# A streamed-weight transformer block on one core: one activation buffer of the MLPs turned into four raw weight tiles and two split pairs

## The chip, the cores and the metric

One core of one Trainium2 chip runs the whole program. The metric is the device time of one execution in microseconds (us), as the median of several runs; lower is better. The engines are TensorE (PE, with PEld for its weight loads), VectorE (DVE), ScalarE (ACT), GpSimd (POOL) and SyncE (SP), and SP's queue issues the weight loads.

## The reference

The input is 256 tokens of width 2048. Layer 0 mixes them with S5 and HGRN2, layer 1 with sliding-window attention, and after each stands an MLP:

```python
def squared_relu_mlp(xn, w_up, w_down):
    return jnp.square(jax.nn.relu(xn @ w_up)) @ w_down

h = x
for layer in range(DEPTH):            # DEPTH = 2
    y = mixer[layer](rms_norm(h, gain[layer]))
    h = h + y
    h = h + squared_relu_mlp(rms_norm(h, mlp_norm[layer]), mlp_w_up[layer], mlp_w_down[layer])
```

`w_up` is 2048 x 8192 and `w_down` 8192 x 2048 in fp32, 64 MB each and twice; together they are two thirds of the 398 MB that the program moves.

## The kernel before

All weights are read once, in one list of **units** that is made before anything runs (`add_units` L80, `add_mlp` L255). A unit is 1024 columns of 128 partitions, 512 KB. Each unit passes three steps:

- its load into a tile `raw` (pool of four, L94), issued by SP at L104, or at L99 where the unit is to be combined with another first;
- its split into two fp32r halves: ACT casts `raw` to `whi` (L129), DVE writes `wlo = raw - whi` (L130); both come from pools of four;
- its matmuls (`mm`, L160), each weight product as hi times hi, hi times lo and lo times hi.

`advance` (L133 to L143) is called once for each unit's matmuls and writes down the loads and splits of later units: loads up to `LOOK_DMA` = 6 units ahead and less than four beyond the last split, splits up to `LOOK` = 3 ahead. The order of each engine's own queue is then set by a scheduler that can put an instruction ahead of others written before it; the waits between engines follow from the tiles. An engine's queue is worked off in order.

The MLP (`mlp` L951) goes through four chunks of 2048 hidden columns. `up(c)` (L971) makes a chunk from 32 units in eight blocks (`ublock`); behind each block ACT and DVE apply the squared ReLU and write the result as a split pair, `ch[c]` with tags `chi` and `clo` (L979 to L986). The pair comes from `new_pair("c")`, which has two buffers, so that chunks alternate. `down(c)` then multiplies the chunk by its rows of `w_down`.

For chunks 0 to 2 `down` is `down_mixed` (L1002), which saves products on part of the work by a seven-product scheme. It follows `down_plan` (L278 to L288), 40 units, which I number idx 0 to 39:

- idx 0 to 17: `t1` (idx 0, 5, 10, 14), `t42` (2, 7, 12, 16) and plain units between them. A `t1` and a `t42` unit have six matmuls each, a plain one 12.
- idx 18 to 31: `b2` (18, 22, 26, 29; six matmuls), `b12` (20, 24, 28, 31; a load of 256 KB, three matmuls) and plain units between them.
- idx 32 to 39: plain units.

That is 84 matmuls of combined units and 24 times 12 = 288 of plain ones, 372 of 512 columns in all. Before the split of a combined unit DVE forms differences on its raw tile (`combine` L108, at L111): one of 512 columns for `t1`, one of 512 and one of 1024 for `t42` (which reads the raw tile of the `t1`), one of 512 for `b12` (which reads that of the `b2`).

Chunk 3 uses `xblock` on 32 plain units. `advance`, `emit_dma`, `emit_split` and `mlp` are what the change touches.

Of the kernel before, what the change touches and what calls it, by code (L numbers as in the profile page):

```python
# [8 lines left out]
F32 = mybir.dt.float32  # L9
F32R = mybir.dt.float32r  # L10
# [7 lines left out]
P = 128  # L18
# [7 lines left out]
LOOK = 3  # L26
WARM = 8
REWARM = 4
LOOK_DMA = 6
# [31 lines left out]
def hybrid_kernel(ctx: ExitStack, tc: tile.TileContext, x, even_norm, even_w_in, s5_lambda_re, s5_lambda_im,  # L61
# [8 lines left out]
    wp = ctx.enter_context(tc.tile_pool(name="wp", bufs=4))  # L70
# [6 lines left out]
    units = []  # L77

    def add_units(W, kts, n0, w=512):
        nk = 1024 // w  # L80
        for i in range(0, len(kts), nk):
            units.append((W, kts[i], n0, nk, None))

    raws, splits = {}, {}
    ptr = {"dma": 0, "split": 0, "use": 0}

    def pieces(i):

        nk = units[i][3]
        return [slice(k, k + 1) for k in range(nk)] if i == 0 else [slice(0, nk)]  # L90

    def emit_dma(i):
        W, kt, n0, nk, kind = units[i]
        raw = wp.tile([P, nk, 1024 // nk], F32, tag="raw", name="raw", bufs=4)  # L94
        raws[i] = raw
        if kind is not None:

            w = 512 if kind == "b12" else 1024
            nc.sync.dma_start(out=raw[:, 0:w // 512], in_=W[kt * P:(kt + 1) * P, n0:n0 + w].rearrange(  # L99
                "p (b n) -> p b n", n=512))  # L100
            return
        src = W[kt * P:(kt + nk) * P, n0:n0 + 1024 // nk].rearrange("(k p) n -> p k n", p=P)
        for ks in pieces(i):
            nc.sync.dma_start(out=raw[:, ks], in_=src[:, ks])  # L104
# [3 lines left out]
    def combine(kind, raw):  # L108

        def sub(o, a, b):  # L110
            V.tensor_tensor(out=o, in0=a, in1=b, op=ALU.subtract)  # L111

        if kind == "t1":
            sub(raw[:, 1], raw[:, 1], raw[:, 0])
        elif kind == "t42":
            sub(raw[:, 0], raw[:, 1], raw[:, 0])
            sub(raw, held["t1"][:, 1:2].to_broadcast([P, 2, 512]), raw)
        elif kind == "b12":
            sub(raw[:, 0], held["b2"][:, 1], raw[:, 0])
        held[kind] = raw  # L120

    def emit_split(i):
        raw, nk, kind = raws.pop(i), units[i][3], units[i][4]
        if kind is not None:
            combine(kind, raw)
        hi = wp.tile([P, nk, 1024 // nk], F32R, tag="whi", name="whi")
        lo = wp.tile([P, nk, 1024 // nk], F32R, tag="wlo", name="wlo")
        for ks in ([slice(0, 1)] if kind == "b12" else pieces(i)):
            S.copy(out=hi[:, ks], in_=raw[:, ks])  # L129
            V.tensor_tensor(out=lo[:, ks], in0=raw[:, ks], in1=hi[:, ks].bitcast(F32), op=ALU.subtract)  # L130
        splits[i] = (hi, lo)

    def advance():  # L133
        i = ptr["use"]
        while ptr["dma"] < min(len(units), i + LOOK_DMA + 1) or ptr["split"] < min(len(units), i + LOOK + 1):
            if ptr["dma"] < min(len(units), i + LOOK_DMA + 1) and ptr["dma"] < ptr["split"] + 4:
                emit_dma(ptr["dma"])
                ptr["dma"] += 1
            else:
                emit_split(ptr["split"])  # L140
                ptr["split"] += 1
        ptr["use"] += 1
        return splits.pop(i)  # L143

# [17 lines left out]
    def wblock(XT, kts, kx=None):  # L162

        acc = psA.tile([P, 4, T], F32, tag="acc", name="acc")
        n = len(kts)
        for i in range(0, n, 2):
            hi, lo = advance()
            for kk in range(2):
                k = kts[i + kk]
                last = i + kk == n - 1  # L170
                for m in range(4):
                    wh, wl = hi[:, kk, m * P:(m + 1) * P], lo[:, kk, m * P:(m + 1) * P]
                    mm(acc[:, m, :], wh, XT.hi[:, k, :], i + kk == 0 and m % 2 == 0, False)
                    mm(acc[:, m, :], wh, XT.lo[:, k, :], False, False)
                    mm(acc[:, m, :], wl, XT.hi[:, k, :], False, last)
            pump(SIDE)
        return acc

    def ublock(XT, kts):

        acc = psA.tile([P, 2, 2, T], F32, tag="acc", name="acc")
        n = len(kts)
        for i in range(0, n, 4):
            hi, lo = advance()
            for kk in range(4):
                k = kts[i + kk]
                for m in range(2):
                    mm(acc[:, m], hi[:, kk, m * P:(m + 1) * P], XT.both[:, :, k, :], i + kk == 0, False)
                for m in range(2):
                    mm(acc[:, m, 0], lo[:, kk, m * P:(m + 1) * P], XT.hi[:, k, :], False, i + kk == n - 1)  # L190
            pump(SIDE)
        return acc
# [42 lines left out]
    def scratch(tag, shape, dtype=F32):  # L235
        return bp.tile(list(shape), dtype, tag=tag, name=tag, bufs=2)
# [14 lines left out]
    for kts in out0_passes:  # L251
        for n in range(4):
            add_units(w_out0, kts, n * 512)

    def add_mlp(l):  # L255
        def up(c):
            for n in range(8):
                add_units(mlp_w_up[l], K16, c * 2048 + n * 256, 256)

        def down(c):  # L260
            if c == 3:
                for n in range(4):
                    add_units(mlp_w_down[l], [c * 16 + k for k in K16], n * 512)
                return
            for kind, n, i in down_plan:
                if kind is None:
                    add_units(mlp_w_down[l], [c * 16 + 2 * i, c * 16 + 2 * i + 1], n * 512)
                else:
                    units.append((mlp_w_down[l], c * 16 + 2 * i + (kind in ("t42", "b2")),
                                  512 if kind == "b12" else 0, 2, kind))  # L270

        for c in range(4):
            up(c)
            down(c)


    NS = 4
# [17 lines left out]
    for kts in out1_passes:  # L295
        for n in range(4):
            add_units(w_out1, kts, n * 512)
    add_mlp(1)


# [40 lines left out]
    for q in range(1, 5):  # L341
        emit_dma(ptr["dma"])
        ptr["dma"] += 1
        load_x(q)
# [17 lines left out]
    for q in range(8):  # L362
        lastx = make_xT(xt, XT0, "g0", 2 * q, 2)
        if q == 0:
            with tc.issue_after(lastx[2].ins):
                for _ in range(REWARM):
                    PE.matmul(wps, warm[:, 0:P], warm, start=True, stop=True, skip_group_check=True)
        if q < 4:
            emit_split(ptr["split"])
            ptr["split"] += 1  # L370
            if q < 3:
                emit_dma(ptr["dma"])
                ptr["dma"] += 1
                load_x(5 + q)
# [576 lines left out]
    def mlp(norm, nxt):  # L951
        XT = norm.XT
        ch, forms = {}, {}
        rst = cp.tile([P, T], F32, tag="rsb", name="rst", bufs=1)

        def row():
# [324 lines left out]
```

## Time and profile before

| what | value |
|---|---|
| median of 3 runs | 2112.44 us (2110.84 to 2113.88) |
| the profiled execution | 2112.92 us |
| its span, first to last instruction | 2110.3 us |
| mean granted TensorE clock | 0.998 |
| PE busy | 2075.3 us (98%) |
| DVE busy | 1481.7 us (70%) |
| ACT busy | 1136.9 us (54%) |
| moved by DMA | 397.75 MB, 188 GB/s over the span |

The profile is of one execution, and sums are made against its own 2112.92 us. Busy times of PE overlap with their neighbours' ends, so a stretch in which PE is busy throughout is told by the rate of its matmuls and by the absence of idle time. Stretches of the span below are called **stages**: an up stage is `up(c)`, a mixed stage is `down_mixed(c)`. The six mixed stages run, by their first matmuls, from 512.40, 694.69, 874.46, 1481.38, 1660.48 and 1839.74 us; the chunk 3 stage of the second MLP is plain and begins at 2019.13 us.

### The profile page before, as it was taken

The page shows a single profiled execution, that of the slowest core. Times are in us where ns is not written, and L with a number is a line of the kernel's source. Part 1 is how long each engine was busy: PE and PEld are TensorE (multiplying, and loading weights), DVE is VectorE, ACT ScalarE, POOL GpSimd, SP SyncE. Part 2 cuts the span into 40 slices and gives each one's busy share as a digit, 9 for nine tenths or more (in the row PEclk, how much of TensorE's full clock was granted, in tenths as well). Part 3 has the DMA queues.
Part 4 walks back from the last instruction along what each step waited for, and adds up shares of the span by engine and source line. Part 5 has one row for each costly group of instructions (what it writes and reads, how often), then busy time and mean ns, then how long its engine had stood idle before and what let it go on. Part 6 is the DMA issues. An engine that isn't in the chain of part 4 may idle for free.

```text
span 2110.3 us, 31236 instructions
## 1 busy us (share of the span) xinstructions
PE 2075.3 (98%) x12144; PEld 1754.9 (83%) x12144; DVE 1481.7 (70%) x2100; ACT 1136.9 (54%) x1541; POOL 38.8 (2%) x38
## 2 busy tenths in 40 slices
PE   9999999999999999999999999999999999999999
PEld 8988988888788878878888888788778878877887
DVE  6799967776666767676655688777767676676654
ACT  5877554565445545544544477565445445544542
POOL 2000000000000000000000110000000000000000
PEclk9999999999999999999999999999999999999999
DMA  8444545566676666566655643456676566567654
GB/s 244 123 150 143 169 159 205 178 182 191 201 223 190 198 231 190 189 220 209 190 189 181 189 149 129 139 175 186 209 230 189 186 230 205 187 214 225 189 200 150
DMA packets 264739, 397.75 MB, mean 188 GB/s; under 512 B 14888, under 2 KB 148560, under 8 KB 264272
## 3 DMA queue, kind: packets, MB, share of 16 engines
q1 hardware_dynamic: 263168, 392.50, 59.0%
q8 instruction: 95, 1.56, 0.3%
q0 software_dynamic: 672, 2.15, 0.3%
q10 hardware_dynamic: 752, 1.12, 0.2%
q14 instruction: 52, 0.43, 0.1%
HBM read 393.62 MB, written 2.10 MB: 188 GB/s over the span
## 4 chain that ended last, share of the span: by engine, by line
PE 78%; DMA 11%; DVE 7%; issue 2%; ACT 2%; SPq 0%; DVEq 0%; ACTq 0%
PE acc L160 65%; PE m L160 12%; DMA raw<-in_mlp_w_down_dram 10%; DVE wlo L130 4%; DVE raw L111 2%; ACT whi L129 1%; PE m L353 1%; PE m L1174 1%; DMA xt<-in_x_dram 0%; DVE t L646 0%; DVE h L1000 0%; PE m L449 0%; DVE clo L986 0%; PE m L1208 0%; ACT chi L627 0%
## 5 line engine op out<-in xcount | busy, mean ns | idle before, releaser
L129 ACT CAST whi<-raw 128x1024 fp32r<-128x1024 f32 (+1 forms) x753 | 777.2, 1036 | 866.8 <-PE acc L160 570.3
L130 DVE TENSOR_TENSOR wlo<-raw,whi 128x1024 fp32r<-128x1024 f32 (+1 forms) x753 | 900.4, 1204 | 443.8 <-ACT whi L129 440.6
L160 PE MATMUL acc<-x,whi 128*128 128x512 f32 (+1 forms) x2816 | 788.1, 366 | 0.2 <-DVE x L357 0.2
L160 PEld LDWEIGHTS acc<-x,wlo 128*128 128x128 f32 x2432 | 458.4, 189 | 91.2
L160 PE MATMUL acc<-x,wlo 128*128 128x256 f32 x2432 | 512.6, 279 | 0.0
L160 PEld LDWEIGHTS acc<-x,whi 128*128 128x128 f32 x2816 | 433.7, 190 | 2.0 <-issue 0.4
L160 PE MATMUL acc<-whi,chi 128*128 128x512 f32 x864 | 338.9, 392 | 0.1
L160 PE MATMUL acc<-wlo,chi 128*128 128x512 f32 x864 | 338.1, 392 | 0.0
L160 PE MATMUL acc<-whi,clo 128*128 128x512 f32 x864 | 338.0, 392 | 0.0
L160 PEld LDWEIGHTS acc<-wlo,chi 128*128 128x128 f32 x864 | 162.6, 188 | 35.4 <-DVE wlo L130 2.0
L160 PEld LDWEIGHTS acc<-whi,chi 128*128 128x128 f32 x864 | 162.3, 188 | 35.5 <-ACT whi L129 1.6
L160 PEld LDWEIGHTS acc<-whi,clo 128*128 128x128 f32 x864 | 162.5, 188 | 33.6
L160 PE MATMUL acc<-whi,x 128*128 128x512 f32 x576 | 181.4, 393 | 0.0
L111 DVE TENSOR_TENSOR raw<-raw 128x512 f32<-128x512 f32 (+1 forms) x96 | 79.1, 824 | 110.9 <-DMA raw<-in_mlp_w_down_dram 110.6
L160 PE MATMUL m<-whi,chi 128*128 128x512 f32 x296 | 112.1, 398 | 14.7 <-ACT whi L129 14.7
L160 PE MATMUL m<-wlo,chi 128*128 128x512 f32 x296 | 116.9, 395 | 9.6 <-DVE wlo L130 9.4
L160 PEld LDWEIGHTS acc<-whi,x 128*128 128x128 f32 x576 | 107.4, 188 | 22.3 <-issue 0.4
L160 PE MATMUL m<-whi,clo 128*128 128x512 f32 x296 | 115.5, 390 | 0.0
L160 PE MATMUL acc<-wlo,x 128*128 128x512 f32 x288 | 113.4, 394 | 0.0
L160 PEld LDWEIGHTS m<-whi,chi 128*128 128x128 f32 x296 | 55.5, 188 | 35.5 <-ACT whi L129 25.1
L160 PEld LDWEIGHTS m<-wlo,chi 128*128 128x128 f32 x296 | 55.6, 188 | 25.5 <-DVE wlo L130 14.7
L160 PE MATMUL m<-whi,forms 128*128 128x512 f32 x192 | 75.3, 392 | 0.0
(243 smaller groups left out, 1560.0 us busy)
## 6 DMA issues: line engine op xcount, KB each, us to landing
raw<-in_mlp_w_down_dram SPq DMA_DIRECT2D x280, 512.0 KB, 4.2
raw<-in_mlp_w_up_dram SPq DMA_DIRECT2D x256, 512.0 KB, 3.7
raw<-in_even_w_in_dram SPq DMA_DIRECT2D x79, 512.0 KB, 3.9
raw<-in_odd_w_qkv_dram SPq DMA_DIRECT2D x40, 512.0 KB, 3.6
raw<-in_even_w_out_dram SPq DMA_DIRECT2D x32, 512.0 KB, 3.9
raw<-in_odd_w_out_dram SPq DMA_DIRECT2D x32, 512.0 KB, 3.8
raw<-in_mlp_w_down_dram SPq DMA_DIRECT2D x24, 256.0 KB, 4.6
raw<-in_s_w_glu_dram SPq DMA_DIRECT2D x8, 512.0 KB, 3.5
```

Source lines behind the costliest of these rows:

```text
L111: V.tensor_tensor(out=o, in0=a, in1=b, op=ALU.subtract)
L129: S.copy(out=hi[:, ks], in_=raw[:, ks])
L130: V.tensor_tensor(out=lo[:, ks], in0=raw[:, ks], in1=hi[:, ks].bitcast(F32), op=ALU.subtract)
L160: PE.matmul(o, a, b, start=start, stop=stop, skip_group_check=True, **kw)
L353: ipe = PE.transpose(ps[:, b, t * P:(t + 1) * P], src[:, t, (a + b) * P:(a + b + 1) * P], ident)
L1174: PE.transpose(ps[:, r, a, :], pr[:, 2 * a + r, k * P:(k + 1) * P], ident)
```

## The change

In an MLP the second buffer of `chi` becomes `more["raw"]`, four raw tiles more, and one buffer of `clo` becomes `more["split"]`, two pairs of split halves more. Units of odd number within the MLP ("home" units) are loaded into the new raw tiles; those whose number is 1 modulo 4 are split into the new pairs. A load may stand ten units ahead (`LOOK_DMA` + 4) and a split five (`LOOK` + 2), as far as their own kind of tile is free. The pair `ch[c]` is left with one buffer. Nothing is computed otherwise.

```diff
+    more = {"from": 0, "end": 0}
+
+    def home(i):
+
+        return more["from"] <= i < more["end"] and i % 2 == 1
+
     def emit_dma(i):
         W, kt, n0, nk, kind = units[i]
-        raw = wp.tile([P, nk, 1024 // nk], F32, tag="raw", name="raw", bufs=4)
+        if home(i):
+            raw = more["raw"][:, i // 2 % 4].rearrange("p (k n) -> p k n", k=nk)
+        else:
+            raw = wp.tile([P, nk, 1024 // nk], F32, tag="raw", name="raw", bufs=4)
         raws[i] = raw
@@ emit_split
-        hi = wp.tile([P, nk, 1024 // nk], F32R, tag="whi", name="whi")
-        lo = wp.tile([P, nk, 1024 // nk], F32R, tag="wlo", name="wlo")
+        if home(i) and i % 4 == 1:
+            hi, lo = [more["split"][:, i // 4 % 2, a].rearrange("p (k n) -> p k n", k=nk) for a in range(2)]
+        else:
+            hi = wp.tile([P, nk, 1024 // nk], F32R, tag="whi", name="whi")
+            lo = wp.tile([P, nk, 1024 // nk], F32R, tag="wlo", name="wlo")
@@ advance
         i = ptr["use"]
-        while ptr["dma"] < min(len(units), i + LOOK_DMA + 1) or ptr["split"] < min(len(units), i + LOOK + 1):
-            if ptr["dma"] < min(len(units), i + LOOK_DMA + 1) and ptr["dma"] < ptr["split"] + 4:
+
+        def room():
+            d = ptr["dma"]
+            if home(d) and d > ptr["split"] + 5:
+                return False
+            return d < min(len(units), i + LOOK_DMA + (4 if home(d) or home(d - 1) else 0) + 1) and sum(
+                home(u) == home(d) for u in raws) < 4
+
+        def ahead():
+
+            u = ptr["split"]
+            if u >= len(units) or u > i + LOOK + 2:
+                return False
+            ext = home(u) and u % 4 == 1
+            return sum((home(v) and v % 4 == 1) == ext for v in splits) < (2 if ext else LOOK + 1)
+
+        while True:
+            if room():
                 emit_dma(ptr["dma"])
                 ptr["dma"] += 1
-            else:
+            elif ahead() and ptr["split"] < ptr["dma"]:
                 emit_split(ptr["split"])
                 ptr["split"] += 1
+            else:
+                break
         ptr["use"] += 1
         return splits.pop(i)
@@ add_mlp: ends.append(len(units)) behind the chunks
@@ mlp
         ch, forms = {}, {}
+        more["raw"] = scratch("chi", [P, 4, 1024])
+        more["split"] = scratch("clo", [P, 2, 2, 1024], F32R)
+        more["from"], more["end"] = ptr["dma"], ends.pop(0)
```

With the change the lines shift: the loads are at L113 and L108, the combine's differences at L120, the subtraction at L142, the matmul at L190, the activation's lines 36 further down.

How the rows of the queues move is shown for the second mixed stage. `raw_N` is a raw tile of the pool, `chi_4782` the four new raw tiles, `clo_4783` the new split pairs, `wlo_N` a pool tile, `m` and `acc` sums in PSUM, `t4` a scratch tile.

SP, loads of that stage, before, idx 3 to 10 of the plan:

```order
L104 DMA raw_6969<-in_mlp_w_down_dram 128x2x512
L104 DMA raw_6992<-in_mlp_w_down_dram 128x2x512
L99 DMA raw_7014<-in_mlp_w_down_dram 128x1024
L104 DMA raw_7051<-in_mlp_w_down_dram 128x2x512
L99 DMA raw_7063<-in_mlp_w_down_dram 128x1024
L104 DMA raw_7082<-in_mlp_w_down_dram 128x2x512
L104 DMA raw_7095<-in_mlp_w_down_dram 128x2x512
L99 DMA raw_7113<-in_mlp_w_down_dram 128x1024
```

And with the change, idx 4, 6, 9, 7, 8, 10, then 13 and 11, then 12, 14:

```order
L113 DMA raw_6814<-in_mlp_w_down_dram 128x2x512
L113 DMA raw_6861<-in_mlp_w_down_dram 128x2x512
L113 DMA chi_4782<-in_mlp_w_down_dram 128x2x512
L108 DMA chi_4782<-in_mlp_w_down_dram 128x1024
L113 DMA raw_6909<-in_mlp_w_down_dram 128x2x512
L108 DMA raw_6961<-in_mlp_w_down_dram 128x1024
L113 DMA chi_4782<-in_mlp_w_down_dram 128x2x512 x2
L108 DMA raw_6994<-in_mlp_w_down_dram 128x1024
L108 DMA raw_7021<-in_mlp_w_down_dram 128x1024
```

Odd units now go to the new tiles, and those that are 1 modulo 4 stand one or two places earlier; a pool tile comes back eight units later instead of four.

DVE in the same stage, before: subtractions of idx 12 to 16 with the differences of idx 14 (`t1`, `raw_7176`) and idx 16 (`t42`, `raw_7214`). The load of idx 16 goes into the tile of idx 12, which the first row here sets free; the difference that reads it stands four places behind:

```order
L130 TENSOR_TENSOR wlo_7199<-raw_7145,whi_7198 128x1024
L111 TENSOR_TENSOR raw_7176<-raw_7176 128x512
L130 TENSOR_TENSOR wlo_7217<-raw_7163,whi_7216 128x1024
L130 TENSOR_TENSOR wlo_7230<-raw_7176,whi_7229 128x1024
L111 TENSOR_TENSOR raw_7214<-raw_7214 128x512
L111 TENSOR_TENSOR raw_7214<-raw_7176,raw_7214 128x1024
L130 TENSOR_TENSOR wlo_7248<-raw_7194,whi_7247 128x1024
L130 TENSOR_TENSOR wlo_7262<-raw_7214,whi_7261 128x1024
```

And with the change: subtractions of idx 8, 10 and 13, the differences of idx 16 (`raw_7053`), the subtractions of idx 11, 12 and 14, the difference of idx 20 (`b12`, `raw_7118`):

```order
L142 TENSOR_TENSOR wlo_7024<-raw_6909,whi_7023 128x1024
L142 TENSOR_TENSOR wlo_7044<-raw_6961,whi_7043 128x1024
L142 TENSOR_TENSOR clo_4783<-chi_4782,clo_4783 128x1024
L120 TENSOR_TENSOR raw_7053<-raw_7053 128x512
L120 TENSOR_TENSOR raw_7053<-raw_7021,raw_7053 128x1024
L142 TENSOR_TENSOR wlo_7068<-chi_4782,whi_7067 128x1024
L142 TENSOR_TENSOR wlo_7083<-raw_6994,whi_7082 128x1024
L142 TENSOR_TENSOR wlo_7103<-raw_7021,whi_7102 128x1024
L120 TENSOR_TENSOR raw_7118<-raw_7078,raw_7118 128x512
```

The load of idx 16 now goes into the tile that the first row here (idx 8) sets free, and that of idx 20 into the tile of idx 12; the difference that reads it stands two places behind.

PE in a mixed stage, before: a plain unit's matmuls (`acc_7069`) and those of the combined unit behind it (`m`) alternate in places:

```order
L160 MATMUL acc_7069<-whi_7097,chi_6243 128x512
L160 MATMUL m_7048<-whi_7117,chi_6243 128x512
L160 MATMUL m_7047<-whi_7117,forms_6245 128x512
L160 MATMUL acc_7069<-wlo_7098,chi_6243 128x512
```

With the change each unit's matmuls stand together:

```order
L190 MATMUL acc_6981<-whi_6977,clo_6186 128x512
L190 MATMUL m_6958<-whi_7004,chi_6185 128x512
L190 MATMUL m_6958<-wlo_7005,chi_6185 128x512
L190 MATMUL m_6958<-whi_7004,clo_6186 128x512
L190 MATMUL m_6957<-whi_7004,forms_6187 128x512
```

The number of matmuls is the same; only which of two neighbouring units comes first at a few places has moved.

## Rows read from the trace of the kernel before

**Rows 1.** Page, part 1: busy time and share by engine

```profile
PE 2075.3 (98%) x12144; PEld 1754.9 (83%) x12144; DVE 1481.7 (70%) x2100; ACT 1136.9 (54%) x1541; POOL 38.8 (2%) x38
```

**Rows 2.** Page, part 4: chain that ended last, by engine, then by line

```profile
PE 78%; DMA 11%; DVE 7%; issue 2%; ACT 2%; SPq 0%; DVEq 0%; ACTq 0%
PE acc L160 65%; PE m L160 12%; DMA raw<-in_mlp_w_down_dram 10%; DVE wlo L130 4%; DVE raw L111 2%; ACT whi L129 1%; PE m L353 1%; PE m L1174 1%; DMA xt<-in_x_dram 0%; DVE t L646 0%; DVE h L1000 0%; PE m L449 0%; DVE clo L986 0%; PE m L1208 0%; ACT chi L627 0%
```

**Rows 3.** Busy time by stretch: mixed stages, an up stage, the plain stage

```profile
core 0: us, PE busy (x) PEld busy (x) DVE busy (x) ACT busy (x) POOL busy (x), PEclk, DMA share, GB/s
512.40:605.53 93.13, 88.07 (x375) 70.50 (x374) 64.08 (x69) 42.67 (x46) 0.00 (x0) 0.98 0.65 215
694.69:785.29 90.60, 86.42 (x374) 69.28 (x373) 63.81 (x69) 42.82 (x46) 0.00 (x0) 1.00 0.68 222
874.46:965.83 91.37, 86.93 (x374) 69.12 (x373) 64.04 (x69) 42.79 (x46) 0.00 (x0) 1.00 0.66 220
1481.38:1571.32 89.94, 86.39 (x375) 69.21 (x373) 63.91 (x69) 42.81 (x46) 0.00 (x0) 1.00 0.68 223
1660.48:1750.58 90.10, 86.39 (x375) 69.21 (x373) 63.91 (x69) 42.89 (x46) 0.00 (x0) 1.00 0.68 222
1839.74:1929.96 90.22, 86.79 (x374) 69.25 (x373) 63.90 (x69) 42.79 (x46) 0.00 (x0) 1.00 0.68 224
785.29:874.46 89.17, 89.17 (x514) 77.81 (x513) 61.72 (x78) 47.62 (x58) 0.00 (x0) 1.00 0.62 188
2019.13:2084.42 65.29, 65.29 (x291) 54.05 (x289) 33.73 (x31) 26.91 (x27) 0.00 (x0) 1.00 0.63 209
770.00:780.00 10.00, 10.00 (x46) 8.29 (x45) 8.28 (x9) 4.63 (x5) 0.00 (x0) 1.00 0.89 285
```

**Rows 4.** Waits in 694.69 to 785.29: us in total, times, longest

```profile
DVE raw L111 <- DMA raw<-in_mlp_w_down_dram: 17.3, 10, 4.2
DVE wlo L130 <- ACT whi L129: 9.8, 7, 2.6
```

**Rows 5.** Waits of SP's queue in the same stretch

```profile
SPq L104 <- DVE wlo L130: 38.7, 25, 5.6
SPq L99 <- DVE raw L111: 11.6, 3, 4.1
```

**Rows 6.** Raw tiles' loads: an up stage (610 to 680 us), then 694.69 to 757.25

```profile
DMA to landing us min/median/max: 3.4/3.7/4.3
...
DMA to landing us min/median/max: 3.1/4.7/5.8
```

**Rows 7.** Chain in 680 to 770: start, us, what

```profile
698.26 3.48 DMA raw<-in_mlp_w_down_dram
...
719.10 4.70 DMA raw<-in_mlp_w_down_dram
...
728.22 5.75 DMA raw<-in_mlp_w_down_dram
```

**Rows 8.** DVE and ACT groups by form in 694.69 to 785.29

```profile
L130 DVE TENSOR_TENSOR wlo<-raw,whi 128x1024 fp32r<-128x1024 f32 x36 | 43.5, 1220 | 10.0 <-ACT whi L129 9.8
L111 DVE TENSOR_TENSOR raw<-raw 128x512 f32<-128x512 f32 x10 | 6.9, 693 | 17.3 <-DMA raw<-in_mlp_w_down_dram 17.3
...
L129 ACT CAST whi<-raw 128x1024 fp32r<-128x1024 f32 x36 | 37.6, 1052 | 43.3 <-DMA raw<-in_mlp_w_down_dram 14.3 <-PE acc L160 9.7 <-DVE raw L111 9.7
```

**Rows 9.** DVE's timeline from 703 us: start, us, instruction

```profile
703.51 1.22 DVE L111 TENSOR_TENSOR raw<-raw 128x1024 f32<-128x1024 f32 x1
704.64 1.22 DVE L130 TENSOR_TENSOR wlo<-raw,whi 128x1024 fp32r<-128x1024 f32 x1
705.78 0.68 DVE L986 TENSOR_TENSOR clo<-t,chi 128x512 fp32r<-128x512 f32 x1
706.38 2.35 DVE L130 TENSOR_TENSOR wlo<-raw,whi 128x1024 fp32r<-128x1024 f32 x2
```

**Rows 10.** Page, part 6: the half loads, KB each, us to landing

```profile
raw<-in_mlp_w_down_dram SPq DMA_DIRECT2D x24, 256.0 KB, 4.6
```

More of the change, by code (lines that the diff above doesn't have):

```diff
@@ L253, in hybrid_kernel @@
             add_units(w_out0, kts, n * 512)
+    ends = []
     def add_mlp(l):
@@ L274, in add_mlp @@
             down(c)
+        ends.append(len(units))
     NS = 4
```

## The prediction

> **What bounds the kernel now.** I read the shares of the page first, then the chain, then the stages, and last the waits of one stage. PE is busy 98% of the span [rows 1], so the most that any change of buffers can give is what PE loses. The chain shows whom it loses it to: 78% PE, but 10% loads of `w_down` and 6% DVE's subtractions and differences [rows 2]. Loads of `w_up` are not in it, though there are as many. So the loss sits in the down stages.
>
> The stretches show how much. In the plain stage 288 matmuls take 65.29 us, 0.2267 us each, with PE busy throughout [rows 3]. An up stage, 89.17 us, is busy throughout too and loses nothing. A mixed stage has 372 matmuls, which at that rate take 84.33 us; the six take 93.13, 90.60, 91.37, 89.94, 90.10 and 90.22. **They lose 8.80, 6.27, 7.04, 5.61, 5.77 and 5.89, together 39.4 us, 6.57 each.** In the first the granted clock is 0.98 on the mean, which is 1.9 of its 8.80; I take this for a consequence of the idling.
>
> The waits of the second mixed stage tell the cause. DVE is busy for 63.8 of 90.60 us, waits 17.3 us in ten pieces for loads that a difference needs, and 9.8 us for casts [rows 3, 4]: 90.9 together, the whole stage. The casts are late since ACT waits 14.3 us for loads and 9.7 us for PE to free a split pair [rows 8]. SP waits in turn for DVE: 38.7 us for subtractions, 11.6 us for differences [rows 5]. This is a ring: a subtraction frees a raw tile, SP issues the load of four units later, that lands in some 4.7 us [rows 6], the difference waits for it at the head of DVE's queue, and the next subtractions stand behind it. A combined unit keeps PE busy for 6 x 0.2267 = 1.36 us only, so four units are little cover. An up stage has four plain units, 10.9 us, against a landing of 3.7 us [rows 6].
>
> **The change part by part.** It removes no instruction on PE, DVE or ACT and adds none; loads are as many, on the same queue. It moves waits.
>
> *Eight raw tiles.* A load waits for the subtraction of eight units before, not four. For plain units that is enough: ACT's waits for loads, and with them the waits of DVE for casts, should go.
>
> *Two more split pairs.* Every fourth unit is split into a pair of its own kind, so that the four pairs of the pool last for more units and ACT waits less for PE. PE has up to five finished units at the start of the stage.
>
> *The differences.* Here the order on DVE says less than the diff. The difference of idx 16 stands two places behind the subtraction that frees its tile, as the order after shows, not eight units behind it; the same holds at six places of the stage (idx 12, 16, 20, 24, 28 and 31). DVE's queue is worked off in order, so **it still waits there**. What it costs I add up from DVE's rows. A 1024-wide operation holds DVE for 1.135 us (703.51 to 704.64 to 705.78) and a 512-wide one for 0.60 us [rows 9]. From the subtraction of idx 4, which the cast of 1.05 us [rows 8] lets begin 1.15 us into the stage, up to that of idx 27, 23 wide and 16 narrow operations stand ahead: 23 x 1.135 + 16 x 0.605 = 35.8 us, and the last ends 1.22 us later, with 38.2 us as the sum. PE wants idx 27 after 240 matmuls, 54.4 us. So DVE has 16.2 us to wait in.
>
> The six waits are each a landing L less what DVE does meanwhile. Between release and difference lie 2.345, 2.27, 1.135, 2.345, 1.74 and 1.74 us of work (one to two wide operations and up to two narrow ones), 11.6 in all; a release comes 0.085 us after the next operation's start (1.22 against 1.135 [rows 9]), 0.5 us in six. The waits are 6L - 11.1, and a stage loses **max(0, 6L - 27.3)**.
>
> What is L with the change? No row shows it, so I bound it. Lower end: 3.48 us, a landing in the chain of this stage, about the 3.7 us of an up stage [rows 6, 7]; then nothing is lost. Upper end: 5.75 us, the longest piece in the chain [rows 7]; then 7.2 us a stage, more than today. I take 4.7 us, the middle of this very stage, where loads come at the same spacing of a DVE operation or two and next to the same neighbours [rows 6]; 4.70 stands in the chain as well [rows 7], and the half loads, which four of the six waits are for, take 4.6 us [rows 10]. Loss: 28.2 - 27.3 = 0.9 us, in six stages 5.4 us. Each 0.1 us of L is worth 3.6 us in the whole kernel.
>
> The Trainium skill has a fit of a transfer's time for the software path, 2.0 us plus bytes by 436e3 a microsecond (DMA: Bandwidth & Descriptors, "Anatomy of one DMA"); as an estimate for these hardware-queued loads it would give 3.2 us for 512 KB. The rows do not agree, and by it the sum would be 2073.5 us.
>
> *One activation buffer.* `up(c+1)` writes `chi` only behind its first block, whose matmuls stand on PE behind all of `down(c)`. An up stage is eight blocks of 11 us, so the write comes long after the last read. Cost zero; without that cover the write would wait for the down stage's end, where it stands anyway.
>
> *The start of an MLP.* The new tiles take the loads of four odd units at once, ahead of loads of the output projection. 2.1 MB at 285 GB/s, the most seen [rows 3], is 7.4 us. A plain unit's load has 10.9 us less a landing of 3.7, or 7.2 us, of cover, and behind it stand finished pairs for 8.2 us. Cost zero, and below 0.4 us for both MLPs if the pairs gave nothing.
>
> *Traffic.* A mixed stage moves 36 loads of 0.524 MB and four of 0.262, 19.9 MB; in 84.33 us that is 236 GB/s, against 222 now and 285 at the most [rows 3]. It does not bind on the mean.
>
> **Sum.** 2112.9 for the profiled execution, less 39.4, plus 5.4: **2079 us** (2078.9). The median stands 0.5 us under that execution, which changes nothing here. A difference of 0.2%, 4.2 us, is about what a measurement of this kernel can tell from none.
>
> **The rivals.**
>
> *Half the gain.* The landings lengthen to about 5.2 us, since DVE, freed of its waits for casts, releases tiles at a faster pace and the loads come in closer groups. 6 x 5.2 - 27.3 = 3.9 us a stage, 23.4 in six: 2097. For it speaks that the middle is 4.7 now but single pieces reach 5.75 [rows 7]; against it that the mean rate rises by 6% only.
>
> *It does not do what it says.* The order on DVE keeps the differences two places behind the releases, DVE has waited 17.3 us for them until now and would wait 6 x 4.7 - 11.1 = 17.1 again. If this ring alone sets the stage, nothing is gained: 2109 to 2117 us. Against it: 63.8 + 17.1 = 80.9 us, and a stage needs 84.33; today's sum is full only with the 9.8 us of waits for casts [rows 4].
>
> *Slower.* More loads stand in the queue at once, and the one that DVE waits for shares its transfer with those of plain units issued ahead of their need. At 285 GB/s a load of 512 KB ahead of it takes 1.84 us; half of one more on each landing of 4.7 is 5.6, a whole one 6.5. I price it at 5.8, the longest of the stage today [rows 6]. Then 34.8 - 27.3 = 7.5 us a stage, 45 in six, 2118.5 us. The point from which it decides is L = 5.65, where the loss is today's 6.57. For it: 5.75 was seen [rows 7], and loads of far units now stand ahead of near ones on SP (idx 9 ahead of 7, 13 ahead of 11). Against it: each load still waits for one subtraction, so the number in flight is set by DVE's pace as before. The Trainium skill speaks against the change at this place: transfers, whoever issues them, run on the same 16 DMA engines and interleave (DMA: Bandwidth & Descriptors, "Issuing engines are not separate DMA queues"); the 0.89 share at 285 GB/s agrees with a shared limit [rows 3].
>
> *Everything gone.* L stays under 4.55 and nothing is lost: 2073.5 us. With a tenth or two between, I don't part this from the forecast; it sets the lower end, with 2.5 us for clock and median.
>
> **How the numbers follow.** The forecast, L up to 5.0 and so 2071 to 2090 us, has 0.57; half the gain, 2090 to 2108, 0.27; no effect, 2109 to 2117, 0.09; slower 0.07. The range 2071 to 2103 leaves out the upper part of the second case (some 0.03) and the last two, and 0.01 below. Faster by over 0.2%: 0.84; within 0.2%: 0.09; slower: 0.07.
>
> **What would show it.** Right: the six mixed stages at 84.5 to 86 us with the up stages at 89.17; DVE's waits for loads at its differences still some 17 us a stage but in six pieces, not ten; waits of DVE for casts and of ACT for loads nearly gone; no load of `w_down` in the chain but a few short pieces; landings near 4.7 us. The clock of the first mixed stage back at 1.00. Wrong: landings over 5 us in the mixed stages, or differences that wait over 20 us a stage; idle time of PE at the first block of an up stage (the single buffer) or at the output projection's end (the four early loads); mixed stages that stay near 90 us though ACT no longer waits for loads.

## The result and the profile after

| what | before | with the change |
|---|---|---|
| median | 2111.64 us (4 runs, 2108.14 to 2113.88) | 2078.21 us (4 runs, 2076.50 to 2080.77) |
| ratio | | 0.9844, 95% interval 0.9825 to 0.9863 |
| span of the profiled execution | 2110.3 us | 2074.9 us |
| predicted | | 2079.0 us (2071 to 2103) |

Ratios, here and below, are taken against executions of the kernel before in the same series. One execution of a run below, the first one of the buffers of before with later differences, took 5797 us at a mean granted clock of 0.35 and stands in no time and no ratio given here.

The stages of the changed kernel, cut at the same matmuls as in [rows 3] (six mixed stages, an up stage; columns as there):

```profile
510.73:596.39 85.66, 85.00 (x375) 69.60 (x373) 60.62 (x66) 42.98 (x46) 0.00 (x0) 1.00 0.72 237
685.55:772.07 86.52, 85.05 (x375) 69.61 (x373) 60.52 (x66) 42.97 (x46) 0.00 (x0) 1.00 0.72 234
861.23:945.87 84.64, 84.64 (x375) 69.77 (x373) 60.52 (x66) 43.01 (x46) 0.00 (x0) 1.00 0.72 237
1461.42:1545.91 84.49, 84.49 (x374) 69.76 (x373) 60.54 (x66) 43.00 (x46) 0.00 (x0) 1.00 0.73 238
1635.08:1719.93 84.85, 84.85 (x375) 69.67 (x373) 60.73 (x66) 43.00 (x46) 0.00 (x0) 1.00 0.74 240
1809.09:1894.23 85.14, 84.70 (x375) 69.68 (x373) 60.74 (x66) 42.98 (x46) 0.00 (x0) 1.00 0.73 240
772.07:861.23 89.16, 89.16 (x513) 77.80 (x512) 64.61 (x82) 47.60 (x58) 0.00 (x0) 1.00 0.61 188
```

The reader is to see that only the mixed stages moved. Their sum is 511.3 us against 545.4, and 506.0 at 84.33 each: of 39.4 us lost, 5.3 are left (1.33, 2.19, 0.31, 0.16, 0.52 and 0.81). The up stages between them last 89.16 us as before, so the single activation buffer costs nothing. From the end of the third mixed stage to the start of the fourth both kernels take 515.55 us, so the start of the second MLP costs nothing either. The granted clock of the first mixed stage is 1.00, 0.98 before. The span fell by 35.4 us, 34.1 of it here; most of the rest lies ahead of the first MLP, where kernels built on either version differ among runs by as much (the first mixed stage begins at 510.7 us here, 512.4 before, and 510.4 in a run below that has the buffers of before).

The waits of the second mixed stage, which answer to [rows 4] and [rows 8] (us in total, times, longest):

```profile
DVE raw L120 <- DMA raw<-in_mlp_w_down_dram: 8.3, 3, 2.8
DVE raw L120 <- issue: 6.5, 2, 3.8
DVE wlo L142 <- ACT whi L141: 6.2, 6, 1.5
...
DVE chi L120 <- issue: 3.2, 1, 3.2
...
DVE clo L142 <- ACT clo L141: 1.5, 1, 1.5
```

ACT's waits for loads, 14.3 us before, have no row any more. DVE's waits at differences did not fall: 8.3 + 6.5 + 3.2 = 18.0 us against 17.3, but in six pieces, not ten. DVE's waits for casts fell from 9.8 to 7.7 us only. Of these, 6.6 us before and 6.8 now come behind the last place of the stage at which PE is held. Those ahead of it fell from 3.2 to 1.0 us; first the two before, then the one that is left:

```profile
731.68 1.22 DVE L130 TENSOR_TENSOR wlo<-raw,whi 128x1024 fp32r<-128x1024 f32 x1 [0.55 <-ACT whi L129]
749.10 1.22 DVE L130 TENSOR_TENSOR wlo<-raw,whi 128x1024 fp32r<-128x1024 f32 x1 [2.63 <-ACT whi L129]
```

```profile
686.61 1.23 DVE L142 TENSOR_TENSOR wlo<-raw,whi 128x1024 fp32r<-128x1024 f32 x1 [0.96 <-ACT whi L141]
```

By these rows the rest of the gain is lead, work done before the stage begins: DVE is busy 60.5 us in the stage against 63.8, and 64.6 in the up stage that follows against 61.7 [rows 3].

Where "issue" stands as the releaser, the load had landed less than 0.1 us before. The six waits on DVE's timeline of that stage (start, us, instruction, idle before it), with one release ahead of its difference:

```profile
692.87 0.69 DVE L120 TENSOR_TENSOR raw<-raw 128x512 f32<-128x512 f32 x1 [2.69 <-DMA raw<-in_mlp_w_down_dram]
...
704.39 1.95 DVE L120 TENSOR_TENSOR raw<-raw 128x512 f32<-128x512 f32 x2 [2.82 <-DMA raw<-in_mlp_w_down_dram]
...
707.40 2.35 DVE L142 TENSOR_TENSOR wlo<-raw,whi 128x1024 fp32r<-128x1024 f32 x2
712.42 0.69 DVE L120 TENSOR_TENSOR raw<-raw 128x512 f32<-128x512 f32 x1 [2.67 <-issue]
...
721.59 0.69 DVE L120 TENSOR_TENSOR raw<-raw 128x512 f32<-128x512 f32 x1 [2.73 <-DMA raw<-in_mlp_w_down_dram]
...
731.30 0.69 DVE L120 TENSOR_TENSOR raw<-raw 128x512 f32<-128x512 f32 x1 [3.80 <-issue]
...
739.22 0.69 DVE L120 TENSOR_TENSOR chi<-chi 128x512 f32<-128x512 f32 x1 [3.22 <-issue]
```

The first subtraction at 707.40 (idx 12) frees the tile that the difference at 712.42 (idx 20) needs, with one other between. That is the order that the diff does not tell. PE stands idle at one place of the stage:

```profile
734.32 0.50 PE L190 MATMUL acc<-wlo,chi 128*128 128x512 f32 x1 [1.33 <-DVE wlo L142]
```

This is idx 23, whose subtraction is the second operation behind the difference of the fifth wait. The matmul that needs the subtraction of idx 27, behind the sixth wait, comes some 0.4 us late besides (742.24 us). The landings of the stage up to idx 31 are told apart by tile, first those into the pool, then those into the new tiles:

```profile
DMA to landing us min/median/max: 3.7/5.4/8.3
```

```profile
DMA to landing us min/median/max: 3.6/4.4/8.5
```

Over the six stages the medians are 4.9 to 5.4 us in the pool and 4.4 to 4.9 in the new tiles; before they were 4.5 to 4.8. The chain of the changed kernel reaches back over a tenth of the span only, all of it PE, so it says nothing of the stages.

### The profile page after: what moved, and what is told of

It is laid out like the page before. It is cut to its first block, busy times and chain, and to the rows that moved or that the text cites. A ratio compares the mean times of both kernels' runs of the same rounds, so it can differ in the third digit from the quotient of the medians.

```text
span 2074.9 us, 31132 instructions
## 1 busy us (share of the span) xinstructions
PE 2062.2 (99%) x12144; PEld 1755.4 (85%) x12144; DVE 1476.6 (71%) x2100; ACT 1137.5 (55%) x1541; POOL 38.8 (2%) x38
## 5 line engine op out<-in xcount | busy, mean ns | idle before, releaser
L141 ACT CAST whi<-raw 128x1024 fp32r<-128x1024 f32 (+1 forms) x479 | 494.1, 1034 | 524.8 <-PE acc L190 427.5
L142 DVE TENSOR_TENSOR wlo<-raw,whi 128x1024 fp32r<-128x1024 f32 (+1 forms) x479 | 571.0, 1200 | 243.5 <-ACT whi L141 242.7
L190 PE MATMUL acc<-x,whi 128*128 128x512 f32 (+1 forms) x2336 | 636.0, 359 | 0.0
L190 PEld LDWEIGHTS acc<-x,wlo 128*128 128x128 f32 x1952 | 367.7, 189 | 70.2 <-DVE wlo L142 0.3
L190 PE MATMUL acc<-x,wlo 128*128 128x256 f32 x1952 | 417.9, 279 | 0.1
L190 PEld LDWEIGHTS acc<-x,whi 128*128 128x128 f32 x2336 | 359.6, 190 | 1.5 <-issue 0.4
L190 PE MATMUL acc<-wlo,chi 128*128 128x512 f32 x664 | 260.1, 392 | 2.6 <-DVE wlo L142 2.4
L190 PE MATMUL acc<-whi,chi 128*128 128x512 f32 x664 | 260.4, 392 | 0.0
L190 PE MATMUL acc<-whi,clo 128*128 128x512 f32 x664 | 259.4, 391 | 0.0
L142 DVE TENSOR_TENSOR wlo<-chi,whi 128x1024 fp32r<-128x1024 f32 x138 | 165.5, 1199 | 108.4 <-ACT whi L141 108.3
L141 ACT CAST whi<-chi 128x1024 fp32r<-128x1024 f32 x138 | 142.5, 1032 | 160.7 <-PE acc L190 123.7
L141 ACT CAST clo<-chi 128x1024 fp32r<-128x1024 f32 x136 | 143.0, 1053 | 137.6 <-PE acc L190 110.0
L142 DVE TENSOR_TENSOR clo<-chi,clo 128x1024 fp32r<-128x1024 f32 x136 | 166.1, 1223 | 58.1 <-ACT clo L141 57.0
L190 PE MATMUL acc<-whi,x 128*128 128x512 f32 x576 | 181.4, 393 | 0.0
L190 PE MATMUL acc<-x,clo 128*128 128x512 f32 x960 | 176.9, 337 | 0.0
L190 PEld LDWEIGHTS acc<-x,clo 128*128 128x128 f32 x960 | 150.2, 188 | 21.3
L190 PEld LDWEIGHTS acc<-wlo,chi 128*128 128x128 f32 x664 | 124.7, 188 | 31.7 <-DVE wlo L142 6.8
L190 PEld LDWEIGHTS acc<-whi,chi 128*128 128x128 f32 x664 | 124.7, 188 | 26.4 <-issue 0.8
L190 PEld LDWEIGHTS acc<-whi,clo 128*128 128x128 f32 x664 | 124.7, 188 | 25.3
L190 PEld LDWEIGHTS acc<-whi,x 128*128 128x128 f32 x576 | 107.4, 188 | 22.4 <-issue 0.4
L190 PE MATMUL acc<-clo,chi 128*128 128x512 f32 x400 | 123.1, 389 | 0.0
L120 DVE TENSOR_TENSOR raw<-raw 128x512 f32<-128x512 f32 (+1 forms) x72 | 59.4, 824 | 89.0 <-DMA raw<-in_mlp_w_down_dram 52.7
```

The lines of the kernel that those rows point to most:

```text
L190: PE.matmul(o, a, b, start=start, stop=stop, skip_group_check=True, **kw)
```

## The experiments

**The two parts apart.** First the new raw tiles without the new pairs (in `emit_split` and `ahead`):

```diff
-        if home(i) and i % 4 == 1:
+        if False:
@@ ahead()
-            if u >= len(units) or u > i + LOOK + 2:
+            if u >= len(units) or u > i + LOOK:
-            ext = home(u) and u % 4 == 1
-            return sum((home(v) and v % 4 == 1) == ext for v in splits) < (2 if ext else LOOK + 1)
+            return len(splits) < LOOK + 1
```

> The change with its four new raw tiles, but with the split pairs of before (four pairs, splits three ahead). Theory (eight raw tiles break the ring of subtraction, load, difference; the pairs only add lead): DVE's waits for loads at its differences fall from some 17 us a mixed stage to about 10, as four differences stand closely behind the release of their tile and two no longer do, and ACT no longer waits for loads; with only three units of lead (6 + 12 + 3 matmuls, 4.8 us, in the second phase) single waits of 3.5 us still reach PE: 1 to 3 us lost a stage, 2080 to 2092 us. Rival A (the pairs matter, since ACT waits for PE to free one): stages stay at 89 to 91 us, 2103 us or more. Rival B (the pairs do nothing at all): 2078, as with the whole change.

Measured: 2105.29 us, ratio 0.9984 (0.9972 to 0.9997). The theory named the right direction and far too much gain. The second mixed stage and its waits:

```profile
690.60:779.36 88.76, 85.31 (x374) 69.52 (x373) 62.13 (x67) 42.66 (x46) 0.00 (x0) 1.00 0.69 230
```

```profile
DVE raw L120 <- DMA raw<-in_mlp_w_down_dram: 10.6, 5, 3.7
...
DVE chi L120 <- DMA chi<-in_mlp_w_down_dram: 3.9, 1, 3.9
...
DVE raw L120 <- issue: 1.8, 1, 1.8
```

DVE waits at seven differences, 16.3 us, not some 10: with the tiles the scheduler moved differences forward, and here too they stand one to four places behind the release. The same waits, with three units of lead instead of five, cost 4.4 us in this stage, twice what they cost in the changed kernel. All six stages lose 33.4 us, with waits at differences of 15.5 to 19.6 us each.

Then the pairs without the tiles (in `emit_dma` and `room`):

```diff
-        if home(i):
+        if False:
@@ room()
-            if home(d) and d > ptr["split"] + 5:
-                return False
-            return d < min(len(units), i + LOOK_DMA + (4 if home(d) or home(d - 1) else 0) + 1) and sum(
-                home(u) == home(d) for u in raws) < 4
+            return d < min(len(units), i + LOOK_DMA + 1) and len(raws) < 4
```

> The change with its two new split pairs, but with the four raw tiles and the load rule of before. Theory: the ring stays. Four tiles, each held for a landing of 4.6 us and some 3.6 us of difference, cast and subtraction, give one unit in 2.05 us, and the first two phases want 32 units in 62.6 us, 1.96 each: some 3 us lost a stage, less a lead of one or two units once, so 2088 to 2106 us, and DVE still waits some 17 us a stage in nine or ten pieces. Rival A (the pairs make the gain): 2078. Rival B (pairs are worth nothing without tiles): 2112.

Measured: 2120.52 us, ratio 1.0044 (1.0028 to 1.0060), slower than before, which none of the three had. The waits of the second mixed stage, and ACT's timeline from 711 us:

```profile
ACT clo L141 <- DMA raw<-in_mlp_w_down_dram: 26.8, 8, 5.0
DVE clo L142 <- ACT clo L141: 11.6, 7, 3.7
DVE raw L120 <- DMA raw<-in_mlp_w_down_dram: 9.7, 6, 2.2
```

```profile
711.25 1.05 ACT L141 CAST clo<-raw 128x1024 fp32r<-128x1024 f32 x1 [4.79 <-DMA raw<-in_mlp_w_down_dram]
712.21 2.00 ACT L141 CAST whi<-raw 128x1024 fp32r<-128x1024 f32 x2
```

The waits at differences shrank to 9.7 us, but a new one came on ACT: the casts into the new pairs stand early in ACT's queue while their loads, four tiles behind, do not come early. At 711.25 one held ACT for 4.79 us, and the two casts behind it then ran at once. So apart the parts gain 5 us and lose 10, and together they gain 33: early splits need early loads, and the waits at differences need the lead.

**The differences taken out**, in the kernel before and in the changed one. The three cases of `combine` are left out (no unit is of kind `none`), so the combined units are used as loaded:

```diff
-        if kind == "t1":
+        if kind == "none":
             sub(raw[:, 1], raw[:, 1], raw[:, 0])
-        elif kind == "t42":
-            sub(raw[:, 0], raw[:, 1], raw[:, 0])
-            sub(raw, held["t1"][:, 1:2].to_broadcast([P, 2, 512]), raw)
-        elif kind == "b12":
-            sub(raw[:, 0], held["b2"][:, 1], raw[:, 0])
```

> The kernel before without the differences of combine: the combined units are split and multiplied as loaded, so this part of the computation is left out. DVE has 11 us a stage less to do and no difference at the head of its queue. Theory (the loss of before is DVE held in order at differences that wait for loads): the ring is shorter by the difference, some 1.8 us a unit against 1.96 wanted, and the mixed stages lose 0 to 2 us: 2074 to 2086 us with the buffers of before. Rival (four tiles and four pairs are too few by themselves, whatever DVE's order): stages still lose 4 us or more, 2098 and up.

> The change without the differences of combine, which are left out of the computation as in the run beside it. Theory: what the changed kernel still loses in its mixed stages (0.2 to 2.2 us each, 5.3 together) is the six waits of DVE at differences; without them all six stages stand at 84.3 to 84.6 us and the time is 2073 us, 4 to 5 under the change. Rival (the rest is lost elsewhere, as at a stage's ends or to contention of loads): 2077 to 2079.

Measured: 2072.31 us (ratio 0.9816, 0.9801 to 0.9830) and 2071.16 us (0.9811, 0.9795 to 0.9827). All twelve mixed stages last 84.33 us. The second stage of each:

```profile
684.24:768.57 84.33, 84.33 (x374) 69.85 (x373) 55.40 (x56) 42.88 (x46) 0.00 (x0) 1.00 0.71 237
```

```profile
683.19:767.52 84.33, 84.33 (x375) 69.84 (x374) 55.55 (x56) 42.98 (x46) 0.00 (x0) 1.00 0.72 236
```

With the buffers of before and no differences nothing is lost, though a load still lands in some 4.8 us: the differences are the whole cause. It may be their work on DVE or their place in its queue; these two runs take out both at once. What the change leaves is theirs too.

**The differences moved.** The change again, and the change with each unit's differences queued on DVE behind the subtraction of two units before it (`issue_after` sets the order on DVE and adds no wait):

```diff
-        if kind is not None:
+        if kind is not None and i - 2 in subs:
+            with tc.issue_after(subs[i - 2]):
+                combine(kind, raw)
+        elif kind is not None:
             combine(kind, raw)
...
-            V.tensor_tensor(out=lo[:, ks], ...)
+            subs[i] = V.tensor_tensor(out=lo[:, ks], ...).ins
```

> The change as it is, beside the next two. All theories: 2078 us, the mixed stages together 4 to 7 us over 506.

> The change with each unit's differences queued on DVE behind the subtraction of two units before it, so that they stand some eight operations behind the release of their tile, not two. Nothing else is moved by hand. Theory (the waits are the landing less what DVE does between release and difference): with 8 us of work between, a landing of 4.6 us is over; the six waits of some 17 us a stage fall below 4, and the mixed stages to 84.3 to 84.7 us: 2073 to 2075 us, 3 to 5 under the change. Rival (with less distance between difference and subtraction DVE waits for casts instead): waits for casts rise by 5 us a stage or more and the time is 2078 or above.

Measured: 2078.74 us (2077.21 to 2083.58, ratio 0.9844, 0.9825 to 0.9864) and 2072.27 us (2071.54 to 2072.59, ratio 0.9809, 0.9792 to 0.9827). The mixed stages of the first lose 9.4 us together in its profiled execution, those of the second none:

```profile
685.44:769.77 84.33, 84.33 (x374) 69.83 (x373) 64.41 (x70) 43.31 (x47) 0.00 (x0) 1.00 0.73 243
```

```profile
DVE wlo L145 <- ACT whi L144: 13.2, 13, 2.3
ACT whi L144 <- PE m L193: 9.1, 8, 1.7
ACT whi L144 <- PE acc L193: 8.6, 6, 2.1
...
DVE clo L145 <- ACT clo L144: 6.4, 5, 1.9
ACT clo L144 <- PE acc L193: 5.9, 5, 1.6
```

DVE has no wait for a load at a difference any more. Its waits for casts did rise, from 7.7 to 19.6 us, as the rival had it, but they cost nothing: ACT in turn waits 23.6 us for PE to free a pair, and then finished units are at hand. The times of the second scatter by 1.1 us, those of the first by 6.4, whose stages lost anything from 0.26 to 2.91 us in one execution, as the loads happened to land. In the second run the differences are all there and cost nothing, so what they cost in the change is their place in the queue.

Then the same order with the new tiles alone, without the pairs:

> The four new tiles without the new pairs, as in the run with tiles alone (2105 us), and each unit's differences queued on DVE behind the subtraction of two units before. Theory (tiles alone failed because DVE still waited 16 us a stage at differences that stand one to four places behind the release of their tile, with three units of lead; distance is all that lacks): waits at differences vanish and the stages come to 84.3 to 85 us, 2072 to 2077 us, as with the whole change in that order. Rival (four split pairs are too few for eight tiles: ACT waits for PE to free one): stages stay above 87 us, 2090 or more.

Measured: 2071.92 us (2071.73 to 2072.16, ratio 0.9826, 0.9811 to 0.9840); every mixed stage 84.33 us. The rival falls: four pairs are enough.

And with the buffers of before, each difference behind the subtraction of one unit before (`subs[i - 1]`), run twice:

> The kernel before, tiles and pairs as they were, with each unit's differences queued behind the subtraction of the unit before it. With four tiles the load of a unit starts only at the subtraction of four units before, so no more than three subtractions and a difference, 3.4 to 4 us, can lie between. Theory (distance is bounded by the number of tiles): the waits at differences shrink from 17 us a stage to 6 to 12 but do not vanish, waits for casts take some of it, as difference, cast and subtraction of one unit follow each other; stages lose 2 to 6 us, 2086 to 2110 us. Rival A (order alone is enough): 2073 to 2076. Rival B (order without tiles does nothing): 2110 to 2116.

> The kernel before with its differences one place later, once more, for its waits by stage, which the first run of it left unread. The three times of that run, 2090.7 to 2094.5 us, are 3 to 3.4 us lost a stage. Theory: waits at differences of 6 to 11 us a stage, each under 2 us, beside 10 us or more of waits for casts. Rival: differences no longer wait for loads at all, and the loss is casts alone (four tiles, four pairs).

Measured: 2090.70 to 2094.54 us in three executions (ratio 0.9925, 0.9906 to 0.9944) and a median of 2089.47 us (0.9918, 0.9901 to 0.9935). The second mixed stage of the second run:

```profile
688.40:775.31 86.91, 85.74 (x374) 69.43 (x373) 65.36 (x70) 42.48 (x46) 0.00 (x0) 1.00 0.70 235
```

```profile
DVE wlo L133 <- ACT whi L132: 21.9, 23, 2.0
ACT whi L132 <- DVE raw L111: 20.4, 10, 3.4
ACT whi L132 <- DMA raw<-in_mlp_w_down_dram: 12.6, 12, 2.3
```

The time came where the theory had it, but the waits did not: no difference of this stage waits for a load, and DVE waits 21.9 us for casts, which wait for differences and loads. That was the rival. DVE's wait moved from the difference to the cast behind it; with four tiles a unit's load, difference, cast and subtraction still follow one another, and 1.8 to 3.6 us a stage are lost. By the ratios, order alone is worth half of what the change gains, tiles alone a tenth.

**The landings lengthened.** The four half loads of a stage made whole:

```diff
-            w = 512 if kind == "b12" else 1024
+            w = 1024
```

> The change with the four half loads of a mixed stage made whole: 512 KB where 256 KB are used, the rest is read and not used. That lengthens four of the six landings that DVE waits for by up to 0.9 us each (0.26 MB at 285 GB/s). Theory, loss = sum of the six landings - 27.3: from some 27.4 now to 29.5 to 31, so 2.2 to 3.7 us a stage and 2087 to 2096 us. Rival (landings are not what sets the rest; the lead hides them): 2078 to 2081.

> The kernel before with the same four whole loads a stage. Theory: every landing stands in its chain, so that the four longer ones add 0.5 to 0.9 us each, 2 to 3.6 us a stage: 2124 to 2133 us. Rival (loads hidden anyway): within 3 us of 2112.

Measured: 2103.91 us (ratio 0.9959, 0.9944 to 0.9974) and 2116.74 us (1.0023, 1.0008 to 1.0038). One megabyte more a stage costs the change 25 us and the kernel before 4. The second mixed stage of the change so altered:

```profile
688.72:778.66 89.94, 85.25 (x375) 69.60 (x373) 60.51 (x66) 42.96 (x46) 0.00 (x0) 1.00 0.71 236
```

```profile
DVE raw L120 <- DMA raw<-in_mlp_w_down_dram: 10.3, 3, 4.5
...
DVE raw L120 <- issue: 7.0, 2, 3.9
...
DVE chi L120 <- DMA chi<-in_mlp_w_down_dram: 4.1, 1, 4.1
```

The six waits are 21.4 us, 3.4 more than in the changed kernel, and the loss 5.61, 3.42 more. The mechanism held and my size was small. On the mean of the six stages the waits at idx 12 and 16 are nearly what they were (2.7 and 2.9 us, 3.0 and 2.7 in the run of the change beside it). Those at idx 20, 24, 28 and 31, whose loads grew, are 4.1, 3.6, 4.2 and 3.9 against 2.4, 2.4, 3.8 and 2.8: 1.1 us more on the mean, up to 1.7, where I had reckoned with 0.9 at the most. That 0.9 was worked out with the highest rate seen, 285 GB/s, and so was no upper end; at the 236 GB/s of this stage 0.26 MB are 1.1 us. For before the expectation was wrong: 0.7 us a stage by the medians, not 2 to 3.6, and its rival, within 3 us of 2112, was missed by a little.

**Another engine for the differences** (`G.tensor_tensor` for `V.tensor_tensor` in `combine`, buffers of before):

> The kernel before with the differences computed by POOL, which is idle 98% of the time, instead of DVE; tiles and pairs as they were. Theory (what costs is that DVE, working in order, is held at a difference while subtractions that are ready stand behind): DVE's head waits are POOL's now and its work falls by 11 us a stage; if POOL takes no more than about 1.5 times DVE's time for a difference, the stages lose 0 to 3 us, 2073 to 2092 us. If POOL is three times slower, the ring of four tiles is as long as before by POOL's own time: 2100 to 2140 us. Rival (the wait for the load itself is what counts, whoever waits): 2110 or more even with a fast POOL.

Measured: 2116.06 us, ratio 1.0039 (1.0025 to 1.0053). Groups of POOL and DVE in the second mixed stage:

```profile
L111 POOL TENSOR_TENSOR raw<-raw 128x512 f32<-128x512 f32 x10 | 15.7, 1568 | 44.2 <-DMA raw<-in_mlp_w_down_dram 29.7 <-DVE t L980 6.5 <-DVE wlo L130 6.5
L111 POOL TENSOR_TENSOR raw<-raw 128x1024 f32<-128x1024 f32 x3 | 8.0, 2679 | 0.2
```

```profile
L130 DVE TENSOR_TENSOR wlo<-raw,whi 128x1024 fp32r<-128x1024 f32 x36 | 46.5, 1312 | 28.6 <-ACT whi L129 28.6
```

POOL takes 1568 ns for a difference, 2.3 times DVE's 693 [rows 8], between the two cases that I had named; the ring of four tiles is lengthened by that, and the run does not tell whose wait counts.

## Why the prediction was right, point by point

- **Where the loss sits, 39.4 us in six stages.** Right: without the differences, and with the differences moved, every mixed stage lasts 84.33 us to the hundredth, the figure worked out from the plain stage.
- **Plain loads no longer wait.** Right: ACT's waits for loads are gone.
- **Waits for casts nearly gone.** Wrong as a sign: 7.7 us of 9.8 are left in the second stage. The prediction took the 9.8 us for what fills today's stage; two thirds of them came behind the last place at which PE is held, so they cost nothing. Those ahead of it went down from 3.2 to 1.0 us, and lead did the rest.
- **The six differences still wait, 6L - 11.1 us.** Right, with one thing to set straight: 11.1 counts from the moment when DVE could take the next operation, 0.085 us before the last one ends [rows 9], and the idle time that the profile shows counts from the end. So the idle time shown is 6L - 11.6. The six waits on the timeline add up to 17.9 us, which makes L = 29.5 / 6 = 4.92 in that stage; over the six stages the waits are 17.1, 17.9, 14.8, 15.9, 16.3 and 16.6, so L is 4.67 on the mean, 4.7 taken.
- **A stage loses what exceeds 16.2 us of waits.** Right: 16.2 us is 15.7 of idle time as shown. The six losses of 1.33, 2.19, 0.31, 0.16, 0.52 and 0.81 are the waits less 15.7, or near nothing where the waits are below; the whole loads, with waits of 20.3 to 23.9, lose 4.56 to 8.11, again the waits less 15.7. PE is held at idx 23, four units ahead of the one that I reckoned with, as well as at idx 27; in the third stage at idx 23 alone, which is why it loses 0.31 us with waits of 14.8.
- **The sum, 5.4 us left.** Measured 5.3, and the closeness is in part luck. With the same L of 4.67 in every stage the sum would be 4.3; the stages spread from 4.40 to 4.92, and the one below 4.55 gives nothing back. The second profiled execution of the change has an L of 4.78 on the mean and loses 9.4 us. And 4.7 was a choice between 3.48 and 5.75 with 3.6 us of time in each 0.1: the mechanism was worked out, the size of L was not.
- **Landings near 4.7 us.** Right for L. The loads of the pool's tiles landed in 4.9 to 5.4 us in the median, over 5 in five of the six stages, which the prediction had named as a sign of being wrong.
- **What stood at no cost**, the single activation buffer, the early loads and the traffic of 236 GB/s: up stages at 89.16 us, 515.55 us from the third mixed stage to the fourth in both kernels, 234 to 240 GB/s in the mixed stages. That the idling brought the clock of the first stage down, as I took it, is not shown: stages at 0.98 or less, here and in the runs, all lose over 5 us, but most stages that lose as much are at 1.00.
- **The rivals.** The slower one needed L at 5.65, which the change never came to. That longer landings would take the gain back is shown by the whole loads: waits of 20.3 us and more, L from 5.3 to 5.9, and 33.4 us lost in six stages, five sixths of the way back. Whether the early loads of plain units lengthened any landing is not shown. "It does not do what it says" failed, as the waits at differences stayed and the time fell. "Half the gain" needed L at 5.2; in the two profiled executions of the change the longest waits of a stage are 18.6 us, L = 30.2 / 6 = 5.03.
- **What the prediction lacked.** It gave the gain to the tiles and counted the pairs as lead beside them. The runs show that neither part does much alone, and that it is the place of the differences that makes lead necessary at all. Nor did it say that ending ACT's waits for loads would not be enough: with three units of lead 16 us at differences cost 4.4 us in the second stage.

In these traces a queue holds what is ready behind what is not, on DVE at differences and on ACT at early casts: 4.79 us at one cast, with two behind it that ran at once. The Trainium skill says in PSUM — Partial Sum Buffer, "Engine vs sequencer instructions", that the queues of ScalarE, VectorE and GpSimd are strict FIFO, and the traces agree.

## What to carry to other kernels

Where loads come back through a ring of tiles, look for the instruction that waits for a load at the head of an in-order queue, and count the work between the release of its tile and it: what the landing exceeds this by is paid every time, first out of the lead and then in time. More tiles help little unless that distance grows with them (2105 us with eight tiles and the old order, 2072 with the new). Moving the instruction behind work that is ready cost no memory of its own and, with the tiles, took all of the loss (2072 us, where the two parts of the change gave 2078); it is worth looking at the order of the queue before buying buffers. And a part of a change that does little alone may still be needed by the other, so part them on the chip before dropping one.

## What the hardware showed that was not expected

While POOL computed differences, DVE's subtractions of 1024 columns took 1312 ns on the mean, 1220 without. The Trainium skill gives a reason in SBUF — State Buffer, "SBUF: two separate sides": DVE with two inputs in SBUF and GpSimd share a pair of ports, held by one for a whole instruction. The rows agree in direction; no run here parts the ports from other causes.

With twice the tiles the loads into the pool did not land sooner but later: in the median 4.9 to 5.4 us in the mixed stages (4.4 to 4.9 into the new tiles), 4.5 to 4.8 before, at 234 to 240 GB/s against 215 to 224. The runs do not part the traffic from the order of the loads.

Still open is why whole loads cost the kernel before so little, 0.7 us a stage, when its chain holds loads throughout [rows 7]; its waits were not parted further. Nor was a lag of two units tried with the four tiles of before.
